# Two-block transformer on one core: the second block's element-wise work taken off POOL, the next heads projected ahead, gates moved forward, meta keys padded

## The chip, the cores and the metric

The kernel runs on one core of one Trainium2 chip. A core has five engines that work side by side, each through its own queue in order: PE (TensorE, matmul), DVE (VectorE), ACT (ScalarE), POOL (GpSimd) and SP (SyncE, here only the issuer of transfers). An engine that waits for one instruction's inputs holds everything queued behind it. The metric is the time of one execution on the device, in microseconds (us).

## The reference, cut to what matters

Two transformer blocks over 256 tokens and a width of 1024 in float32. The first (a mixer with banded attention and retention, then an MLP) keeps its instructions. The second prepends 16 learned meta tokens, projects once by `w_in`, and joins two kinds of attention by gates:

```python
def second_block(x, meta_tokens, pre_mix_gain, w_in, ...):
    h = jnp.concatenate([filler, meta, x], axis=1)
    ...
        u = rms_norm(h, pre_mix_gain[l])
        proj = u @ w_in[l]
        qa, ka, va, qb, kb, vb, g = jnp.split(proj, SPLITS, axis=-1)
        qa = rope(qa.reshape(B, Lp, SWA_Q_HEADS, HEAD_DIM), pos)
        ka = rope(ka.reshape(B, Lp, SWA_KV_HEADS, HEAD_DIM), pos)
        qb = rope(qb.reshape(B, Lp, DIFF_HEADS, 2, HEAD_DIM), pos)
        kb = rope(kb.reshape(B, Lp, DIFF_HEADS, 2, HEAD_DIM), pos)
        o_swa = windowed_gqa_sink_attention(qa, ka, va, attn_sink[l], pos, is_real)
        ...
        o_diff = differential_attention(qb, kb, vb, lam, ...)
        gates = jax.nn.sigmoid(g + b_gate[l])
        g_swa, g_diff = gates[..., :D_MODEL], gates[..., D_MODEL:]
        merged = g_swa * (o_swa @ w_branch_swa[l]) + g_diff * (o_diff @ w_branch_diff[l])
        h = h + rms_norm(merged @ w_out[l], post_mix_gain[l])
        ...
```

A gated feed-forward layer follows. The banded attention (16 query heads of 64, 4 key heads) lets a query see keys within 128 positions, all 16 meta keys, and a sink logit without a value: softmax over `[band, meta, sink]`. The differential attention (8 heads of two halves) is `(softmax(q1 k1) - lam * softmax(q2 k2)) @ v` over all 272 keys, with a norm per head. `rope` turns each pair of half heads: `[x1 c - x2 s, x2 c + x1 s]`.

## The kernel before

**Weights and matmuls.** Every matmul of weights is done in three passes over two parts of each number (high by high, high by low, low by high). The weights come as a stream of 272 units of 1024x128 (512 KB, laid out as 128x1024). `fetch` (L286 to L305) brings one: a transfer on SP's queue into one of four `raw` buffers, two casts on ACT to `hi` (L302), two subtractions on DVE to `lo` (L304), into one of five pairs of buffers. The units are used in the order in which `pack_weights` lays them. A unit over 256 tokens is 24 matmuls of 256 columns (L459), over 272 tokens 24 of 272. Queries, gates and branch products take two units at a time, called a block below: 48 matmuls.

**Ropes.** `rope_T` (L495 to L517) copies the projection from PSUM on ACT (`t`, L506 or L508), issues four transfers on ACT's queue that swap the half heads (`sw<-t`, L510, L511), multiplies by the cosines on DVE (L512), multiplies the swapped tile by the sines (L513) and adds (L516) on `self.slow`, which is POOL in the second block (set at L927) and DVE in the first. Keys are tiles of 128x272, queries of 128x512. `stack_q` (L519 to L528) splits the queries into high parts (ACT) and low parts (`self.slow`, L526, L527); `stack_k` (L529 to L544) does so for keys (`ks` on ACT, `kl` on DVE at L541 and on POOL at L542).

**Banded attention** (loop at L980): four chunks `c` of four heads, two query tiles each, so eight calls of `sink_attention` (L599 to L638). Per head: two score matmuls `s<-ks` and `s<-kl`; one matmul of 128 columns in bf16 that adds the mask (L566); on DVE the sink is copied into column 272 (L577) and the minimum taken (L571; queries are scaled by -0.125, so the minimum is the largest logit); exponentials with their sum on ACT (L581); reciprocal and scaling on DVE (L583, L584) to `pn`. Per tile of four heads: transposes (L620), a split into high and low (L331 with L330 on ACT), products `o_ps` (L624), with the third key tile of 16 rows only, then `ol` on ACT (L629), `of` on DVE (L631) and the split of the result into `os_t`. A second form, `sink_softmax1` (L586), which the first block uses, adds the mask and takes the minimum in one custom DVE instruction (L591) and scales on ACT (L597).

**Differential attention** (L990 to L1055): four pairs `pr` of heads; each begins with `keys()` (two units, two key tiles) and the queries, and ends with one gate block of the first kind (L1055). **Branches** (L1061 to L1072): four blocks `bs` on the banded result, then four times a gate block of the second kind (L1068) and a block `bd` on the differential result (L1069), their sum on POOL (L1071) and a split into `m2t`. The output projection `op` follows at 687 us, then the feed-forward layer.

**What sets the order.** The code is written out head by head, and a scheduler orders each engine's queue from it when the kernel is built, within the buffers that each tile has (`BUFS`) and the PSUM banks (`ROT`). That order is fixed.

## Time and profile before

| what | value |
|---|---|
| time, median of 3 runs | 903.83 us (902.67 to 905.01) |
| the profiled execution, its own time | 906.26 us |
| its span, first to last instruction | 904.5 us |
| PE busy in the span | 881.3 us, 97% |
| DVE busy | 628.5 us, 69% |
| ACT busy | 521.4 us, 58% |
| POOL busy | 152.8 us, 17% |
| mean granted clock of PE | 0.994 |

Shares over the whole span mix stages with different limits. The stages that the change touches lie between 426 us (first key projection of the second block) and 687 us (first output projection), and are read apart below. A busy PE is not PE at its peak: the records of its matmuls overlap, so their paces are read from long rows of equal matmuls in the chain.

### The profile page before, as it was taken

The page shows a single profiled execution, that of the slowest core. Times are in us where ns is not written, and L with a number is a line of the kernel's source. Part 1 is how long each engine was busy: PE and PEld are TensorE (multiplying, and loading weights), DVE is VectorE, ACT ScalarE, POOL GpSimd, SP SyncE. Part 2 cuts the span into 40 slices and gives each one's busy share as a digit, 9 for nine tenths or more (in the row PEclk, how much of TensorE's full clock was granted, in tenths as well). Part 3 has the DMA queues.
Part 4 walks back from the last instruction along what each step waited for, and adds up shares of the span by engine and source line. Part 5 has one row for each costly group of instructions (what it writes and reads, how often), then busy time and mean ns, then how long its engine had stood idle before and what let it go on. Part 6 is the DMA issues. An engine that isn't in the chain of part 4 may idle for free.

```text
span 904.5 us, 16459 instructions
## 1 busy us (share of the span) xinstructions
PE 881.3 (97%) x6172; PEld 812.4 (90%) x6172; DVE 628.5 (69%) x1203; ACT 521.4 (58%) x1145; POOL 152.8 (17%) x174
## 2 busy tenths in 40 slices
PE   7999999999999999999989999999999999999997
PEld 5899999998899999978978888889998799999996
DVE  5567798768655555665699999988666776656654
ACT  4644389546654444555657778887455554444542
POOL 2001110110011111111464525461110100000000
PEclk9999999999999999999989999999999999999999
DMA  8665754468476655654653343434467576655641
GB/s 294 221 211 167 216 163 154 146 211 305 161 218 192 194 186 189 207 189 148 187 168 98 112 131 108 138 107 133 147 185 241 180 231 188 187 186 187 188 162 46
DMA packets 48320, 160.25 MB, mean 177 GB/s; under 512 B 6497, under 2 KB 8417, under 8 KB 48242
## 3 DMA queue, kind: packets, MB, share of 16 engines
q1 hardware_dynamic: 43378, 153.49, 53.3%
q10 hardware_dynamic: 4672, 5.20, 2.1%
q8 instruction: 48, 0.79, 0.4%
q0 software_dynamic: 192, 0.52, 0.2%
q14 instruction: 30, 0.25, 0.1%
HBM read 151.38 MB, written 2.10 MB: 170 GB/s over the span
## 4 chain that ended last, share of the span: by engine, by line
PE 37%; DVE 8%; DMA 2%; ACT 2%; issue 1%; POOL 1%; ACTq 0%; POOLq 0%; DVEq 0%
PE fi_ps L459 13%; PE op L471 6%; PE gate_ps L459 4%; DVE lo L304 3%; PE bd_ps L459 2%; PE bs_ps L459 2%; PE q_ps L459 2%; PE k_ps L459 2%; DMA raw<-in_wstream_dram 2%; PE o_ps L624 1%; DMA sw<-t 1%; ACT hi L302 1%; PE pt_ps L620 1%; PE fi_ps L481 1%; PE s L563 1%
## 5 line engine op out<-in xcount | busy, mean ns | idle before, releaser
L304 DVE TENSOR_TENSOR lo<-raw,hi 128x512 fp32r<-128x512 f32 x536 | 372.8, 736 | 188.9 <-ACT hi L302 183.8
L302 ACT CAST hi<-raw 128x512 fp32r<-128x512 f32 x532 | 301.9, 618 | 229.2 <-issue 82.1
L471 PE MATMUL op<-hi,hid 128*128 128x512 f32 x416 | 128.9, 390 | 0.0
L459 PE MATMUL fi_ps<-xf2t,hi 128*128 128x256 f32 x640 | 114.4, 281 | 0.0
L459 PEld LDWEIGHTS fi_ps<-xf2t,hi 128*128 128x128 f32 x640 | 99.1, 188 | 0.9
L459 PE MATMUL fi_ps<-xf2t,lo 128*128 128x256 f32 x320 | 90.0, 281 | 0.0
L471 PEld LDWEIGHTS op<-hi,hid 128*128 128x128 f32 x416 | 76.3, 188 | 14.6
L471 PE MATMUL op<-lo,hid 128*128 128x512 f32 x208 | 81.1, 392 | 0.0
L459 PE MATMUL f_ps<-xf1t,hi 128*128 128x256 f32 x448 | 80.5, 281 | 0.0
L459 PEld LDWEIGHTS f_ps<-xf1t,hi 128*128 128x128 f32 x448 | 69.9, 189 | 1.2
L459 PE MATMUL f_ps<-xf1t,lo 128*128 128x256 f32 x224 | 63.0, 281 | 0.0
L459 PEld LDWEIGHTS fi_ps<-xf2t,lo 128*128 128x128 f32 x320 | 60.6, 189 | 0.0
L459 PE MATMUL q_ps<-x2t,hi 128*128 128x256 f32 x256 | 51.6, 292 | 0.0
L459 PE MATMUL gate_ps<-x2t,hi 128*128 128x256 f32 x256 | 48.7, 284 | 0.0
L459 PE MATMUL gate_ps<-x1t,hi 128*128 128x256 f32 x256 | 47.1, 283 | 0.0
L471 PEld LDWEIGHTS op<-lo,hid 128*128 128x128 f32 x208 | 39.0, 188 | 8.6
L459 PEld LDWEIGHTS f_ps<-xf1t,lo 128*128 128x128 f32 x224 | 42.4, 189 | 0.1
L459 PEld LDWEIGHTS q_ps<-x2t,hi 128*128 128x128 f32 x256 | 41.6, 194 | 0.7 <-issue 0.5
L853 POOL TENSOR_TENSOR sq<-relu 128x512 f32<-128x512 f32 x14 | 15.8, 1132 | 150.5 <-ACT relu L850 150.5
L419 POOL TENSOR_SCALAR e<-ss 128x1 f32<-128x1 f32 (+1 forms) x11 | 3.4, 312 | 220.1 <-ACT py L1092 191.8
L459 PEld LDWEIGHTS gate_ps<-x2t,hi 128*128 128x128 f32 x256 | 40.0, 189 | 0.5 <-issue 0.5
L459 PEld LDWEIGHTS gate_ps<-x1t,hi 128*128 128x128 f32 x256 | 39.6, 189 | 0.2
(323 smaller groups left out, 2008.2 us busy)
## 6 DMA issues: line engine op xcount, KB each, us to landing
raw<-in_wstream_dram SPq DMA_DIRECT2D x272, 512.0 KB, 3.7
sw<-t ACTq DMA_DIRECT2D x40, 64.0 KB, 4.0
x<-in_x_dram SPq DMA_DIRECT2D x3, 512.0 KB, 6.0
sw<-t ACTq DMA_DIRECT2D x40, 34.0 KB, 2.1
sw<-t ACTq DMA_DIRECT2D x8, 128.0 KB, 4.8
g_pre<-in_gains_dram SPq DMA_DIRECT2D x2, 512.0 KB, 7.0
...
```

What stands on the lines that cost most here:

```text
L302: nc.scalar.copy(hi[:, c:c + PIECE], raw[:, c:c + PIECE])
L304: nc.vector.tensor_sub(lo[:, c:c + PIECE], raw[:, c:c + PIECE], hi[:, c:c + PIECE].bitcast(F32))
L419: nc.gpsimd.tensor_scalar(out=e[:np_], in0=ss[:np_, 0:1], scalar1=1.0 / D, scalar2=EPS, op0=ALU.mult, op1=ALU.add)
L459: nc.tensor.matmul(out, wv[a][:, k, j * P:(j + 1) * P], XT[:, b, k, n0:n1], start=(i == 0), stop=(i == last))
L471: nc.tensor.matmul(out, XT[:, b, k0 + k, t0:t1], wv[a][:, k, c0:c0 + cn], start=(start and i == 0), stop=(stop and i == last))
L481: nc.tensor.matmul(out, XT[:, b, kn * j + k, t0:t1], ws[j][a][:, k, :cn], start=(i == 0), stop=(i == len(seq) - 1))
L563: nc.tensor.matmul(out, q, k[0][:, k0:k1], start=True, stop=False)
L620: nc.tensor.transpose(b[:kn, h, :], pn[:, h, k0:k0 + kn], self.ident)
L624: nc.tensor.matmul(o, vs[i][:kn, c, :], pt[:kn, x], start=(i == 0 and x == 0), stop=(i == len(ktiles) - 1 and x == 1))
L853: nc.gpsimd.tensor_tensor(out=q, in0=r, in1=r, op=ALU.mult)
```

## The change

- `self.slow` stays DVE in the second block, so the S-product and the sum of each rope and the low halves of the queries are on DVE. Half of the keys' low parts (`kl`, L542) stay on POOL.
- The banded attention uses the form of the first block: masks are a table `masks2` (128x544, one transfer on SP), added to the scores in the custom instruction that also takes the minimum; the mask matmuls, the sink copies and the separate minimum go; the scaling of `pn` goes from DVE to ACT. POOL copies the sinks (128x4 per tile).
- Queries of the next chunk, and keys and queries of the next pair, are projected one ahead; `ks` and `kl` get eight buffers for six.
- The first two gate blocks of the first kind stand ahead of the last banded chunk instead of in pairs 0 and 1; the four of the second kind stand ahead of the `bs` products, into tiles that the `pt` tiles used. The last sum goes from POOL to DVE.
- The third key tile is filled with zeros to 128 rows (tiles `va` and, for the transposed weights, `ptm`, cleared once by two memsets on POOL).

The diff, without imports, plain renames and context:

```diff
-    "b2": dict(vt=4, sw=2, t1=2, t2=2, ks=6, kl=6, qe=2, qo=2, p=6, a=2, at=1, atm=2, y=1, pn=2, pt=2),
-    "b3": dict(gt=4),
+    "b2": dict(sw=2, t1=2, t2=2, ks=8, kl=8, qe=2, qo=2, p=6, a=2, at=1, atm=2, y=1, pn=2, pt=2),
...
+
+    def kq(p):
+        in_a(w_in2, o_kb + 256 * p)
+        in_a(w_in2, o_qb + 256 * p)
+    in_a(w_in2, o_qa)
     for c in range(4):
-        in_a(w_in2, o_qa + 256 * c)
+        if c < 3:
+            in_a(w_in2, o_qa + 256 * (c + 1))
+        else:
+            kq(0)
+            in_a(w_in2, o_g)
+            in_a(w_in2, o_g + 256)
         if c == VB1:
             in_a(w_in2, o_vb + 512)
             in_a(w_in2, o_vb + 768)
     for p in range(4):
-        in_a(w_in2, o_kb + 256 * p)
-        in_a(w_in2, o_qb + 256 * p)
-        in_a(w_in2, o_g + 256 * p)
+        if p < 3:
+            kq(p + 1)
+        if p > 1:
+            in_a(w_in2, o_g + 256 * p)
+    for g in range(4):
+        in_a(w_in2, o_g + 1024 + 256 * g)
     for g in range(4):
         in_a(w_bs, 256 * g)
     for g in range(4):
-        in_a(w_in2, o_g + 1024 + 256 * g)
         in_a(w_bd, 256 * g)
     for g in range(4):
...
+    add("masks2", np.concatenate([z, le, z[:, :NMETA], ge, z, z[:, :NMETA]], axis=1))
...
-        mk = self.wp.tile([P, UC], F32, tag="raw", bufs=4, name="mk")[:, 0:2 * P]
-        a, n = cc["masks"]
-        nc.sync.dma_start(out=mk, in_=io["consts"][:, a:a + n])
-        self.identb = cp.tile([P, P], BF16, name="identb")
-        self.masks = cp.tile([P, 2 * P], BF16, name="masksb")
-        nc.gpsimd.tensor_copy(self.identb, self.ident)
-        nc.gpsimd.tensor_copy(self.masks, mk)
...
-        nc.tensor.matmul(out, q, k[1][:, k0:k1], start=False, stop=(mask is None))
-        for i, (mi, c0) in enumerate(mask or ()):
-            nc.tensor.matmul(out[:, c0:c0 + P], self.identb, self.masks[:, mi * P:(mi + 1) * P],
-                             start=False, stop=(i == len(mask) - 1))
+        nc.tensor.matmul(out, q, k[1][:, k0:k1], start=False, stop=True)
...
-    def sink_softmax(self, s, n, nsink, out):
-        nc = self.nc
-        nc.vector.tensor_copy(s[:, n:n + 1], nsink)
-        nm = self.row_min(s)
-        p = self.t([P, NKEY + 2], "p")
-        den = self.sm(1, "den")
-        nc.scalar.activation(out=p[:, :n + 1], in_=s, func=AF.Exp, bias=nm, scale=-1.0, accum_out=den)
-        rc = self.sm(1, "rc")
-        nc.vector.reciprocal(rc, den)
-        nc.vector.tensor_scalar(out=out, in0=p[:, :n], scalar1=rc, scalar2=None, op0=ALU.mult)
-
-    def sink_softmax1(self, s, n, mask, nsink, p):
+    def sink_softmax(self, s, n, mask, nsink, p):
...
-    def sink_attention(self, q, kst, vs, sink, ktiles, masks, OT, c, qt):
...
-        if isinstance(masks, list):
-            pn = self.t([P, 4, n], "pn")
-            for h in range(4):
-                s = self.sbank([P, n + 1], "s")
-                self.scores(s[:, :n], q[h % 2][:, h // 2, qt * P:(qt + 1) * P], kst, 0, n, masks)
-                self.sink_softmax(s, n, sink[:, 4 * c + h:4 * c + h + 1], pn[:, h, :])
-        else:
-            pn = self.t([P, 4, n + 1], "pn")
-            nc.gpsimd.tensor_copy(pn[:, :, n], sink[:, 4 * c:4 * c + 4])
-            for h in range(4):
-                s = self.sbank([P, n], "s")
-                self.scores(s, q[h % 2][:, h // 2, qt * P:(qt + 1) * P], kst, 0, n)
-                self.sink_softmax1(s, n, masks, sink[:, 4 * c + h:4 * c + h + 1], pn[:, h, :])
+        pn = self.t([P, 4, n + 1], "pn")
+        nc.gpsimd.tensor_copy(pn[:, :, n], sink[:, 4 * c:4 * c + 4])
+        for h in range(4):
+            s = self.sbank([P, n], "s")
+            self.scores(s, q[h % 2][:, h // 2, qt * P:(qt + 1) * P], kst, 0, n)
+            self.sink_softmax(s, n, mask, sink[:, 4 * c + h:4 * c + h + 1], pn[:, h, :])
         o = self.pv([P, 4, P], "o_ps")
         for i, (k0, kn) in enumerate(ktiles):
             b = self.tp([P, 4, P], "pt_ps")
             for h in range(4):
                 nc.tensor.transpose(b[:kn, h, :], pn[:, h, k0:k0 + kn], self.ident)
-            pt = self.t([P, 2, 4, P], "pt", F32R)
+            pt = self.t([P, 2, 4, P], "pt", F32R) if kn == P else self.ptm[qt]
             self.split(pt[:kn, 0], pt[:kn, 1], b[:kn])
             for x in range(2):
-                nc.tensor.matmul(o, vs[i][:kn, c, :], pt[:kn, x], start=(i == 0 and x == 0),
+                nc.tensor.matmul(o, vs[i][:, c, :], pt[:, x], start=(i == 0 and x == 0),
                                  stop=(i == len(ktiles) - 1 and x == 1))
         of = self.t([P, 2, P], "of")
-        if isinstance(masks, list):
-            ol = self.t([64, 4, P], "ol")
-            nc.scalar.copy(ol, o[64:128])
-            for e in range(2):
-                nc.vector.tensor_add(of[64 * e:64 * e + 64], o[0:64, e:4:2], ol[:, e:4:2])
-        else:
-            for e in range(2):
-                r = slice(64 * e, 64 * e + 64)
-                nc.scalar.copy(of[r], o[64:128, e:4:2])
-                nc.vector.tensor_add(of[r], o[0:64, e:4:2], of[r])
+        for e in range(2):
+            r = slice(64 * e, 64 * e + 64)
+            nc.scalar.copy(of[r], o[64:128, e:4:2])
+            nc.vector.tensor_add(of[r], o[0:64, e:4:2], of[r])
...
-        self.slow = nc.gpsimd
         rope_b = self.load("rope_b", [P, 2 * NKEY])
+        mk = self.load("masks2", [P, 2 * NKEY], rp)
+        mk = [mk[:, 0:NKEY], mk[:, NKEY:]]
...
-        vat = self.bp.tile([P, 3, 4, P], F32R, tag="A", name="va")
+        vat = self.bp.tile([P, 7, 4, P], F32R, tag="A", name="va")
+        nc.gpsimd.memset(vat[:, 0].bitcast(F32), 0.0)
+        nc.gpsimd.memset(vat[:, 3:7].bitcast(F32), 0.0)
+        self.ptm = [vat[:, 3:5], vat[:, 5:7]]
...
-                f = self.t([P, NKEY], "vt")
+                f = self.t([P, NKEY], "vt", tag="kl")
...
-            va[i] = v
+            va[i] = vat[:, i]
...
+        def queries():
+            return self.stack_q(self.rope_T(self.proj_a(XT, name="q_ps"), 2, NTOK, rope_b, 32, scale=-0.125))
+
         OS = self.big("C", 8, "os_t", NKEY)
         MS = self.bp.tile([P, 8, NTOK], F32, tag="D", name="ms")
         self.banks("WINDOW")
         ka = keys()
+        qn = queries()
         for c in range(4):
-            q = self.stack_q(self.rope_T(self.proj_a(XT, name="q_ps"), 2, NTOK, rope_b, 32, scale=-0.125))
+
+            q = qn
+            if c < 3:
+                qn = queries()
+            else:
+                kn = keys()
+                qn = queries()
+                for g in range(2):
+                    self.gate(XT, 16, g, MS[:, 2 * g:2 * g + 2, :])
             for qt in range(2):
-                self.sink_attention(q, ka[c], va, self.nsink[:, 8:24], kts, [(0, P)] if qt == 0 else [(1, 0)],
-                                    OS, c, qt)
+                self.sink_attention(q, ka[c], va, self.nsink[:, 8:24], kts, mk[qt], OS, c, qt)
...
         for pr in range(4):
-            kb = keys()
-            q = self.stack_q(self.rope_T(self.proj_a(XT, name="q_ps"), 2, NTOK, rope_b, 32, scale=-0.125))
+            kb, q = kn, qn
+            if pr < 3:
+                kn = keys()
+                qn = queries()
...
-            self.gate(XT, 16, pr, MS[:, 2 * pr:2 * pr + 2, :])
-        es.close()
-        es = ExitStack()
-        self.use(es.enter_context(self.phase("b3")), "b3")
+            if pr > 1:
+                self.gate(XT, 16, pr, MS[:, 2 * pr:2 * pr + 2, :])
...
+        gts = [self.t([P, 2, 4, P], "gd", tag="pt") for _ in range(2)]
+        gts = [t.rearrange("p a b c -> p (a b c)").rearrange("p (g m n) -> p g m n", g=2, m=2) for t in gts]
+        for gq in range(4):
+            self.gate(XT, 24, gq, gts[gq // 2][:, gq % 2])
...
         for gq in range(4):
-            tg = self.t([P, 2, 2, NTOK], "gt")
-            self.gate(XT, 24, gq, tg[:, 0])
+            tg = gts[gq // 2][:, gq % 2]
             b = self.proj_a(OD, name="bd_ps")
-            nc.vector.scalar_tensor_tensor(out=tg[:, 1], in0=tg[:, 0], scalar=1.0, in1=b, op0=ALU.add, op1=ALU.mult)
-            nc.gpsimd.tensor_tensor(out=tg[:, 0], in0=tg[:, 1], in1=MS[:, 2 * gq:2 * gq + 2, :], op=ALU.add)
-            self.split(MT[:, 0, 2 * gq:2 * gq + 2, 0:NTOK], MT[:, 1, 2 * gq:2 * gq + 2, 0:NTOK], tg[:, 0], 0.5)
+            nc.vector.scalar_tensor_tensor(out=tg, in0=tg, scalar=1.0, in1=b, op0=ALU.add, op1=ALU.mult)
+            nc.vector.tensor_add(tg, tg, MS[:, 2 * gq:2 * gq + 2, :])
+            self.split(MT[:, 0, 2 * gq:2 * gq + 2, 0:NTOK], MT[:, 1, 2 * gq:2 * gq + 2, 0:NTOK], tg, 0.5)
```

What this does to the queues, at three places. First POOL, where the second block's first ropes stand: `sw`, `t` are the S-product and the sum, `qe`, `qo` the low halves of queries, `kl` those of keys. Before:

```order
L513 TENSOR_TENSOR sw<-sw,rope_b 128x512
L516 TENSOR_TENSOR t_5068<-t_5068,sw 128x512
L513 TENSOR_TENSOR sw<-sw,rope_b 128x512
L516 TENSOR_TENSOR t_5332<-t_5332,sw 128x512
L526 TENSOR_TENSOR qe<-t_5068,qe 64x512
L527 TENSOR_TENSOR qo<-t_5068,qo 64x512
L513 TENSOR_TENSOR sw<-sw,rope_b 128x512
L526 TENSOR_TENSOR qe<-t_5332,qe 64x512
L527 TENSOR_TENSOR qo<-t_5332,qo 64x512
```

After, from the first sink copies on:

```order
L595 COPY pn<-nsink 128x4 x2
L548 TENSOR_TENSOR kl<-t_4922,ks 64x272 x2
L548 TENSOR_TENSOR kl<-t_4978,ks 64x272 x2
L595 COPY pn<-nsink 128x4
L548 TENSOR_TENSOR kl<-t_5994,ks 64x272
L595 COPY pn<-nsink 128x4
L548 TENSOR_TENSOR kl<-t_5994,ks 64x272
L595 COPY pn<-nsink 128x4 x2
```

Only the sink copies, the `kl` and (not shown) the `rq` of the differential heads are left there.

Next DVE in the first chunk, near the third query rope. `lo` are weight units, `s`, `mn`, `rc`, `pn` the softmax. Before:

```order
L512 TENSOR_TENSOR t_5596<-t_5597,rope_b 128x512
L304 TENSOR_TENSOR lo_5986<-raw_5987,hi_5985 128x512 x2
L577 COPY s<-nsink 128x1 x2
L571 TENSOR_REDUCE mn<-s 128x1
L577 COPY s<-nsink 128x1
L304 TENSOR_TENSOR lo_6219<-raw_6220,hi_6218 128x512
L571 TENSOR_REDUCE mn<-s 128x1 x2
L304 TENSOR_TENSOR lo_6219<-raw_6220,hi_6218 128x512
L583 RECIPROCAL rc<-den 128x1 x3
```

After (`ISA` with `masks` is the custom instruction, the one behind it reads its minimum):

```order
L582 ISA pn,mn<-s,masks_4679,nsink 128x272
L582 ISA mn 128x1
L532 TENSOR_TENSOR qe<-t_5148,qe 64x512
L582 ISA pn,mn<-s,masks_4679,nsink 128x272
L582 ISA mn 128x1
L533 TENSOR_TENSOR qo<-t_5148,qo 64x512
L582 ISA pn,mn<-s,masks_4679,nsink 128x272
L582 ISA mn 128x1
L317 TENSOR_TENSOR lo_5874<-raw_5875,hi_5873 128x512
L519 TENSOR_TENSOR sw<-sw,rope_b 128x512
L317 TENSOR_TENSOR lo_5909<-raw_5910,hi_5908 128x512 x2
L587 RECIPROCAL rc<-den 128x1
```

The low halves and the S-product now stand between the heads' softmax on DVE; the copies, minima and scalings are gone.

Last PE in the banded heads. Before, where pair 0's keys begin (`masksb` is the mask matmul):

```order
L563 MATMUL s<-ks,qo 128x272
L564 MATMUL s<-kl,qo 128x272
L566 LDWEIGHTS identb
L566 MATMUL s<-masksb,identb 128x128
L459 MATMUL k_ps<-x2t,hi_6218 128x272
L563 MATMUL s<-ks,qe 128x272
L564 MATMUL s<-kl,qe 128x272
L566 LDWEIGHTS identb
L566 MATMUL s<-masksb,identb 128x128
```

After, in the third chunk:

```order
L604 MATMUL pt_ps<-ident,pn 128x128 x4
L569 MATMUL s<-ks,qe 128x272
L570 MATMUL s<-kl,qe 128x272
L604 MATMUL pt_ps<-ident,pn 16x128 x4
L604 MATMUL pt_ps<-ident,pn 128x128 x3
L569 MATMUL s<-ks,qo 128x272
L570 MATMUL s<-kl,qo 128x272
L604 MATMUL pt_ps<-ident,pn 128x128
L569 MATMUL s<-ks,qe 128x272
L570 MATMUL s<-kl,qe 128x272
L569 MATMUL s<-ks,qo 128x272
L570 MATMUL s<-kl,qo 128x272
```

The mask matmuls are gone. Before, projections stand between the heads' scores; after, this piece holds scores, transposes and products alone. The projections of pair 0 and the first gates stand ahead of the last chunk.

## Rows read from the trace of the kernel before

**Rows 1.** Stretches: length; busy PE, PEld, DVE, ACT, POOL; clock; DMA; GB/s.

```profile
426.00:492.00 66.00, 62.62 (x475) 59.60 (x473) 54.22 (x105) 40.91 (x94) 29.18 (x23) 0.95 0.56 172
492.00:584.00 92.00, 88.42 (x645) 78.45 (x645) 87.87 (x201) 74.09 (x184) 43.94 (x38) 1.00 0.40 117
584.00:647.50 63.50, 61.00 (x520) 59.94 (x519) 50.82 (x119) 44.14 (x137) 19.49 (x20) 1.00 0.39 122
647.50:687.20 39.70, 39.70 (x338) 39.70 (x337) 25.41 (x35) 20.52 (x39) 4.83 (x3) 1.00 0.61 185
687.20:904.00 216.80, 210.34 (x1390) 191.98 (x1388) 132.55 (x238) 103.70 (x213) 6.43 (x13) 0.99 0.56 180
```

**Rows 2.** Tile `os_t` on DVE: duration in ns, first and last start.

```profile
L331 DVE TENSOR_TENSOR os_t<-of,os_t x8: 403/424/1504, 492.0 to 584.1; 128x256 fp32r<-128x256 f32 x8
```

**Rows 3.** Chain that ended last, 640 to 700: start, length, matmuls.

```profile
647.62 5.67 PE bd_ps L459 x48
653.29 5.68 PE gate_ps L459 x48
```

**Rows 4.** DVE groups, 426 to 647.5: count; busy, mean ns; idle before.

```profile
L304 DVE TENSOR_TENSOR lo<-raw,hi 128x512 fp32r<-128x512 f32 x97 | 81.2, 869 | 10.4 <-ACT hi L302 10.3
L584 DVE TENSOR_SCALAR pn<-p,rc 128x272 f32<-128x272 f32 x32 | 15.7, 518 | 0.2
...
L571 DVE TENSOR_REDUCE mn<-s 128x1 f32<-128x273 f32 x32 | 13.1, 428 | 0.1
...
L577 DVE COPY s<-nsink 128x1 f32<-128x1 f32 x32 | 4.3, 148 | 0.4 <-PE s L566 0.4
```

**Rows 5.** DVE groups, 50 to 130, the first block.

```profile
L513 DVE TENSOR_TENSOR sw<-sw,rope_a 128x512 f32<-128x512 f32 x2 | 1.4, 688 | 2.2 <-DMA sw<-t 2.2
...
L591 DVE CUSTOM_DVE_ANT_0 pn<-s,masks,nsink 128x256 f32<-128x256 f32 x1 | 0.5, 481 | 0.0
```

**Rows 6.** Timeline of DVE, 457 to 467: start, length.

```profile
460.80 1.79 DVE L512 TENSOR_TENSOR t<-t,rope_b 128x512 f32<-128x512 f32 x1
```

**Rows 7.** Timeline of POOL in the same window.

```profile
460.41 1.64 POOL L513 TENSOR_TENSOR sw<-sw,rope_b 128x512 f32<-128x512 f32 x1
```

**Rows 8.** Timeline of DVE, 415 to 425; idle before in brackets.

```profile
419.25 4.91 DVE L304 TENSOR_TENSOR lo<-raw,hi 128x512 fp32r<-128x512 f32 x8 [4.26 <-ACT hi L302]
```

**Rows 9.** Timeline of DVE at the first and the eighth `os_t`.

```profile
490.40 0.63 DVE L584 TENSOR_SCALAR pn<-p,rc 128x272 f32<-128x272 f32 x2
...
584.82 0.44 DVE L512 TENSOR_TENSOR t<-t,rope_b 128x272 f32<-128x272 f32 x1 [0.27 <-ACT t L506]
```

**Rows 10.** POOL groups, 426 to 647.5.

```profile
L542 POOL TENSOR_TENSOR kl<-t,ks 64x272 fp32r<-64x272 f32 x20 | 19.2, 960 | 14.2 <-ACT ks L539 13.4
L513 POOL TENSOR_TENSOR sw<-sw,rope_b 128x512 f32<-128x512 f32 x8 | 12.4, 1548 | 29.2 <-DMA sw<-t 15.7 <-DVE pt L331 5.6 <-PE od_ps L1038 3.9
...
L1047 POOL TENSOR_TENSOR rq<-ms,nhalf 128x2 f32<-128x2 f32 x8 | 5.8, 729 | 31.9 <-DVE ms L1045 31.9
```

**Rows 11.** ACT groups, 110 to 150, the first block.

```profile
L597 ACT ACTIVATE pn<-pn,rc 128x256 f32<-128x256 f32 x5 | 2.4, 504 | 0.1
```

**Rows 12.** Timeline of PE, 534.3 to 536, around a product of 16 rows.

```profile
534.89 0.28 PE L459 MATMUL gate_ps<-x2t,lo 128*128 128x256 f32 x1
535.10 0.49 PE L624 MATMUL o_ps<-pt,va 16*128 16x512 f32 x1
535.52 0.50 PE L459 MATMUL gate_ps<-x2t,hi 128*128 128x256 f32 x2
```

**Rows 13.** Timeline of PE, 577 to 582: the last banded product.

```profile
580.24 0.50 PE L624 MATMUL o_ps<-pt,va 16*128 16x512 f32 x1
```

**Rows 14.** Waits of DVE, 50 to 130: us, times, longest.

```profile
DVE sw L513 <- DMA sw<-t: 7.7, 5, 2.2
```

**Rows 15.** Stretches around a low clock, columns as in the first group.

```profile
460.00:467.00 7.00, 4.99 (x40) 4.67 (x38) 7.00 (x9) 2.11 (x6) 6.69 (x5) 1.00 0.32 98
467.00:475.00 8.00, 7.34 (x35) 6.69 (x36) 6.85 (x24) 4.38 (x16) 0.10 (x1) 0.57 0.62 196
```

More of the change, by code (lines that the diff above doesn't have):

```diff
@@ L11 @@
 F32R = mybir.dt.float32r
-BF16 = mybir.dt.bfloat16
 AF = mybir.ActivationFunctionType
```

8 lines of the change are left out of this document (5 added, 3 removed).

## The prediction

> **What bounds the kernel now.** I read the busy time by stretch first [rows 1]. The change lies between 426 and 687 us: banded attention with the key and query projections (to the eighth split of its output `os_t`, 584.1 us [rows 2]), differential attention, and the branch products up to 687.2. What follows, 687 to 904, and all before 426 keep their instructions. From 492 to 584 DVE is busy 87.87 of 92.00 us, 95.5%, with 201 instructions; PE's 88.42 there is overlapped records, not matmuls at their pace. Summing every matmul between 426 and 687 at its pace (0.118 us for 256 columns, 5.68/48 in [rows 3], larger ones in proportion) gives about 241 us of PE work in 261.2, so PE loses about 20. It loses none in 647.5 to 687.2, where PE is busy throughout [rows 1] and the chain is `gate` and `bd` blocks of 48 matmuls back to back [rows 3]. So the middle has two bounds in turn: DVE until banded attention is done, then PE.
>
> Why DVE is full is in the groups. `lo` takes 869 ns over 97 instructions [rows 4], where an undisturbed 128x512 two-operand instruction takes 688 [rows 5]. The timeline shows why: `t` of 128x512 took 1.79 us at 460.80 while POOL's `sw` ran 1.64 us from 460.41 [rows 6, 7]. The excess is 97 x 0.18 = 18 us in `lo`, 32 x (0.518 - 0.355) = 5 us in `pn` (0.355 is its duration undisturbed, below), and some 13 us over the other groups compared in the same way: about 36 us of stall between 426 and 647.5, 14.4, 16.3 and 6.7 us in the three stretches. POOL is busy 29.18 + 43.94 + 19.49 = 92.6 us there [rows 1], so a POOL microsecond costs DVE about 0.39.
>
> **The change part by part.** Records of one engine overlap: eight `lo` in a row took 4.91 us [rows 8], 0.60 each against durations of 0.68, so a pitch is the duration less 0.08.
>
> *POOL's work goes to DVE.* Per rope the S-product and the sum, per query the two low halves. That is 8 ropes of 512 columns, 10 of 272, and 16 low halves: 32 x 0.60 [rows 5] + 20 x 0.35 (0.44 less 0.08 [rows 9]) = 26.2 us more on DVE. POOL keeps 20 `kl` of 0.96 and 8 `rq` of 0.73 [rows 10], 25 us, so stalls fall from 36 to 0.39 x 25 = 10. The two cancel almost exactly.
>
> By the row of one instruction instead of this mean, each `kl` would hold DVE for its whole 0.96 us; that is a rival below. The Trainium skill, "SBUF — State Buffer", section "Who interferes with whom", says that a DVE instruction with two SBUF inputs contends with a GpSimd instruction that reads SBUF and that the lock is held for the whole instruction. The 1.79 us agrees with that; the mean of 0.39 says that few of POOL's instructions meet such a partner for their whole length.
>
> *Mask, sink and minimum in one instruction, scaling to ACT.* Gone from DVE are 32 `s` copies (0.07), 32 `mn` reductions (0.35) and 32 `pn` scalings ((0.63 - 0.08)/2 = 0.275, the pair undisturbed in [rows 9]): 22 us. Instead come 32 custom instructions of 272 columns; 256 took 481 ns in the first block [rows 5], so 0.42 at the pitch: 13.6 us. DVE's net over both parts is 26.2 - 22 + 13.6 = 17.9 us, less 26 of stalls: -8. ACT gains 32 scaled copies; the 256-wide one takes 504 ns [rows 11], about 0.42 at the pitch: 13.3 us, 14.5 with the split of `of` into two.
>
> *PE loses little.* 32 mask matmuls of 128 columns go, about 0.06 each: 1.8 us. The padding of the 16 meta-key rows makes the 16-row products full. The 16-row product starts 0.21 us after the matmul before it and holds the next one 0.42 [rows 12], against 0.118 and 0.236: 0.28 each, 16 of them, 4.6 us. I take both as gone; if the pause belongs to something else, 4.6 us of PE comes back, much of it under DVE's cover. The two memsets stand on POOL ahead of the last `sq` of the first block, whose inputs come later than POOL is free: nothing.
>
> *The order.* Counting the schedule between markers at these pitches: **to the first `os_t`** DVE has 36.1 us of work before and 56.2 after. Ten more `lo` (6.0), nine S-products and nine sums (8.8), eight low halves (4.8), one more query and key rope with two `kl` (1.7), 16 custom instructions (6.8) and small ones (0.9) come in, and 13 reductions, 12 scalings and 14 copies (8.9) leave. With projecting ahead, the second chunk's queries stand before the first chunk's products. **First to eighth `os_t`:** 69.4 before, 71.8 after: two `lo`, 20 scalings, 18 reductions and 18 copies go, 16 custom instructions, 6 low halves and 17 rope instructions come. The count before, times 1.03, plus 16.3 of stalls is 87.8, the busy time in the row [rows 1], so the count carries. **PE from the last banded product (580.2 us [rows 13]) to the first `bd` (647.6):** 63.5 before, 78.1 after. 133 more matmuls of 256 columns (181 of gates, less 48 of queries) at 0.118 are 15.7, and 13 key matmuls less take 1.6 off, and four scores more add 0.5. **`bd` to `op`:** 39.7 before, 22.7 after, since three gate blocks (17.0 us, [rows 3]) have gone forward.
>
> *The sum.* In 426 to 492 DVE idles 66 - 54.2 = 11.8 us; it gets 20.1 x 1.03 = 20.7 more work, 12 us less stall (2 of the 14.4 stay, for six `kl`), and I let its idle shrink to about 7, since the projections now feed it earlier: the first `os_t` comes at 492 + 20.7 - 12.4 - 4.5 = 496. Then 71.8 x 1.03 = 74 plus 6 of stalls is 80, at the present share of 95.5% it is 83.8: the eighth `os_t` at 579.8, 4.3 us earlier than 584.1, and the last banded product, four us ahead of it, likewise. From there PE is the bound: 78.1 plus 1.5 lost, since gate matmuls now fill the gaps between the differential heads, against 67.4 now (63.5 and 3.9 lost), 12.2 more; then 22.7 plus 0.3 against 39.7, 16.7 less. Together -4.3 + 12.2 - 16.7 = **-8.8 us** at `op`; the rest is as before. The profiled run took 906.26 us with a span of 904.5, the median is 903.83; I take the difference off the median: **895 us**.
>
> **The rivals.** *Better, about 884.* The order interleaves so well that half of PE's loss goes too: PE's work falls to 235 us, so with 6 us lost instead of 17 the middle ends 11 us earlier still. For it: 94 gate matmuls and the next keys lie between the banded heads. Against it: PE's order has a stretch with scores, transposes and products only, where DVE has 20 us of work for 12 of PE's.
>
> *No change, 901 to 906.* ACT becomes co-bound. It was busy 74.09 of 92 [rows 1]; it gets 17 scaled copies for its share (7 us) and loses some exponentials and casts, 76.4, and with about 3.5 us of transfer issues 80 of 84. A head now goes PE, DVE, ACT, DVE, ACT, PE, four hand-offs between two engines that are both full. If the share of DVE drops from 95.5 to 88%, 80 takes 91 us and 7 of the 8.8 are gone. With each of the 12 `kl` in this stretch at 0.96 instead of 0.37 us DVE has 7 us more, 87/0.955 = 91, and the time is 902; I give this 0.04 of the chance below. The same range holds the case that the stall does not come from POOL but from DVE's own full queue: then 16 us stay, 90/0.955 = 94, about 905.
>
> *Slower, about 910.* The S-product on DVE waits for the swapped halves, which come by transfer (`sw<-t`), and DVE works in order: `lo`, the softmax and every split queue behind it, and PE behind those. In the first block, where DVE does it already, DVE waited five times, 7.7 us in all [rows 14], for six ropes of 512 columns: 1.3 each. 18 ropes would be 23 us. It decides against the change once such waits before the eighth `os_t` exceed 8.8 us, and passes the 0.3% beyond 11.5; 23 us less the 8.8 and what runs under PE's cover gives 910 and up to 917. Against it: one chunk or pair is projected ahead, so the order puts other DVE work between the transfer's issue and the S-product. POOL waits for these transfers now, 15.7 us before the 512-wide `sw` alone [rows 10], and little queues behind it.
>
> One more cost lies in the range: the granted clock was 0.57 on the mean in 467 to 475, so that PE ran at 1.2 instead of 2.4 GHz for most of it, 0.43 x 8 = 3.4 us lost at the most [rows 15], after a thin stretch (4.99 of 7 us busy in 460 to 467). The thin stretch of the new order could bring a second such fall, and the first may go.
>
> **How the numbers follow.** About 0.3%, 2.7 us either way of 903.83 (901.1 to 906.5), is what a measurement can tell from no change. Forecast 888.5 to 901: 0.60. Better, near 884: 0.12. No change, 901 to 906.5: 0.16. Slower, near 910: 0.12. So faster 0.72, same 0.16, slower 0.12. Eight in ten: from 886, inside the better case, to 905, inside the no-change case.
>
> **What would show it.** Right: `lo` near 0.72 instead of 0.87 us; POOL's busy time in the middle near 26; the first `os_t` at 494 to 498, the eighth at 577 to 583; four `bd` blocks back to back in 22.7 us; `op` at 676 to 681. Wrong: DVE idle before `sw` for the transfer of over 9 us in all; `lo` still at 0.85; ACT over 95% busy in the banded stretch with DVE waiting for `p`; PE idle or at half clock between the eighth `os_t` and `bd`.

## The result, and the profile after

The changed kernel took 897.84 us (897.41 to 898.27, 3 runs) against 903.83 before: a ratio of 0.9935, 95% interval 0.9916 to 0.9953, 6.0 us less. Timed again with more runs (below) it was 0.9921, 0.9904 to 0.9939, 896.94 against 904.23, 7.3 us less. The forecast was 895, -8.8 us, in a range of 886 to 905. The profiled execution took 897.84 us with a span of 895.9, 8.6 less than the span before.

Busy time by stretch, with the bounds at the first and the eighth `os_t`, the first `bd` and `op`, as in [rows 1]; columns are length, then busy PE, PEld, DVE, ACT and POOL with counts, granted clock, DMA share and GB/s:

```profile
426.00:504.50 78.50, 77.76 (x630) 76.34 (x629) 64.41 (x144) 60.28 (x143) 6.15 (x8) 1.00 0.56 179
504.50:591.80 87.30, 78.19 (x577) 71.81 (x577) 78.27 (x191) 78.00 (x195) 17.04 (x16) 0.98 0.39 122
591.80:655.80 64.00, 64.00 (x551) 63.78 (x550) 48.20 (x121) 44.96 (x137) 9.26 (x10) 1.00 0.41 133
655.80:678.50 22.70, 22.70 (x195) 22.70 (x194) 16.62 (x26) 11.04 (x19) 0.00 (x0) 1.00 0.57 185
678.50:895.30 216.80, 210.13 (x1390) 191.98 (x1388) 132.15 (x239) 103.46 (x213) 5.40 (x12) 1.00 0.54 180
```

The last stretch is as long as before (216.8), and from the first key projection (426.0 us before, 426.8 after) to `op` it took 251.7 us instead of 261.2, so the difference lies there. The stretch of the `bd` blocks went from 39.7 to 22.7 us. The chain there answers to [rows 3]: start, length, matmuls.

```profile
655.92 22.72 PE bd_ps L465 x192
```

192 matmuls in 22.72 us, 0.118 each, without a gap. From the last banded product to there PE has no gap either: that product is the last line below (timeline of PE, [rows 13] before), so the tail takes 655.9 - 577.6 = 78.3 us, where the count of matmuls at their pace was 78.1.

```profile
577.60 0.39 PE L608 MATMUL o_ps<-va 128*128 128x512 f32 x1
```

The heads ahead of it are another matter. PE by stretches of 10 us:

```profile
520.00:530.00 10.00, 7.88 (x57) 6.86 (x56) 9.33 (x25) 7.94 (x21) 1.11 (x2) 1.00 0.57 189
530.00:540.00 10.00, 7.45 (x50) 6.23 (x48) 6.53 (x22) 9.83 (x27) 0.19 (x1) 1.00 0.11 30
540.00:550.00 10.00, 7.54 (x38) 5.90 (x38) 9.48 (x28) 9.15 (x26) 3.65 (x4) 0.83 0.17 55
```

Here PE is busy 22.9 of 30 us by the records, and some 19 at the pace of its matmuls; the clock fell to 0.83 in the last slice. DVE and ACT together fill the stretch, one or the other is busy 29.2 of the 30 us, each with a gap while the other works: ACT is at 9.83 of 10 where DVE has 6.53.

DVE's groups from 424 to 650 (count; busy, mean ns; idle before them), to be laid beside [rows 4]:

```profile
L317 DVE TENSOR_TENSOR lo<-raw,hi 128x512 fp32r<-128x512 f32 x108 | 71.8, 697 | 6.3 <-ACT hi L315 6.1
L582 DVE CUSTOM_DVE_ANT_0 pn<-s,masks,nsink 128x272 f32<-128x272 f32 x32 | 14.9, 491 | 0.5 <-PE s L570 0.3
...
L547 DVE TENSOR_TENSOR kl<-t,ks 64x272 fp32r<-64x272 f32 x20 | 11.2, 560 | 0.3
...
L519 DVE TENSOR_TENSOR sw<-sw,rope_b 128x272 f32<-128x272 f32 x10 | 4.4, 436 | 9.5 <-DMA sw<-t 9.4
```

`lo` fell from 869 to 697 ns: nearly all of the stall is gone. In its place stands the last line's idle time, 9.5 us of waiting for the swapped halves. DVE's waits in 426 to 592 (us, times, longest):

```profile
DVE sw L519 <- DMA sw<-t: 10.9, 6, 3.4
DVE lo L317 <- ACT hi L315: 4.2, 5, 1.6
DVE pt L344 <- ACT pt L343: 3.6, 2, 3.3
```

POOL's groups from 424 to 650 ([rows 10] before):

```profile
L548 POOL TENSOR_TENSOR kl<-t,ks 64x272 fp32r<-64x272 f32 x20 | 23.1, 1154 | 62.8 <-ACT ks L545 31.1 <-issue 23.5 <-PE s L570 7.0
L1043 POOL TENSOR_TENSOR rq<-ms,nhalf 128x2 f32<-128x2 f32 x8 | 7.5, 934 | 53.0 <-DVE ms L1041 44.2 <-ACT ks L545 8.7
```

### The profile page after: what moved, and what is told of

Same layout as the page of the kernel before. It is cut to its first block, busy times and chain, and to the rows that moved or that the text cites. A ratio compares the mean times of both kernels' runs of the same rounds, so it can differ in the third digit from the quotient of the medians.

```text
span 895.9 us, 16370 instructions
## 1 busy us (share of the span) xinstructions
PE 870.4 (97%) x6140; PEld 808.4 (90%) x6140; DVE 615.9 (69%) x1227; ACT 535.6 (60%) x1185; POOL 87.9 (10%) x126
## 5 line engine op out<-in xcount | busy, mean ns | idle before, releaser
L317 DVE TENSOR_TENSOR lo<-raw,hi 128x512 fp32r<-128x512 f32 x536 | 352.3, 696 | 177.9 <-ACT hi L315 170.9
L465 PE MATMUL gate_ps<-x2t,hi 128*128 128x256 f32 x256 | 50.6, 285 | 0.0
L465 PE MATMUL q_ps<-x2t,hi 128*128 128x256 f32 x256 | 47.2, 282 | 0.0
L465 PEld LDWEIGHTS q_ps<-x2t,hi 128*128 128x128 f32 x256 | 39.7, 188 | 0.3 <-ACT t L512 0.2
L465 PE MATMUL gate_ps<-x2t,lo 128*128 128x256 f32 x128 | 36.4, 284 | 0.0
L465 PE MATMUL gate_ps<-x1t,lo 128*128 128x256 f32 x128 | 36.2, 283 | 0.0
```

The costliest lines, as they stand in the source:

```text
L317: nc.vector.tensor_sub(lo[:, c:c + PIECE], raw[:, c:c + PIECE], hi[:, c:c + PIECE].bitcast(F32))
L465: nc.tensor.matmul(out, wv[a][:, k, j * P:(j + 1) * P], XT[:, b, k, n0:n1], start=(i == 0), stop=(i == last))
```

## The experiments

Each kernel is timed beside runs of the kernel before on the same chip; those had medians of 903.5 to 904.4 us, so two rows can differ by 0.9 us for that reason alone. Beside the times stands one number that I worked out from the trace of the profiled execution as the prediction did: PE time lost between 426 us and `op`, which is the wall time less the sum of all matmuls at their paces (the products of 16 rows at the pace of 128).

| kernel | median us | against 896.94 | PE lost, us |
|---|---|---|---|
| before | 903.83 | +6.9 | 24.8 |
| changed, again | 896.94 | | 15.9 |
| POOL's work back on POOL | 907.71 | +10.8 | 26.2 |
| key ropes alone back on POOL | 900.33 | +3.4 | 17.4 |
| before, with POOL's work on DVE | 907.51 | +10.6 | 25.5 |
| no padding | 899.33 | +2.4 | 17.6 |
| gates back | 901.90 | +5.0 | 19.6 |
| nothing projected ahead | 900.47 | +3.5 | 21.0 |
| scaling back on DVE | 899.56 | +2.6 | 19.9 |
| last `kl` on DVE too | 900.30 | +3.4 | 20.6 |
| four gate blocks ahead of the last chunk | 897.17 | +0.2 | 14.4 |
| two ahead of the third, two of the last | 896.77 | -0.2 | 15.3 |
| no swap transfers | 886.57 | -10.4 | 4.7 |

A profiled execution can lie up to 2.5 us off its median (902.05 us with the scaling back on DVE, 898.66 with the key ropes on POOL); the times of the profiled executions follow PE's loss to within 2 us. Except where the text says so the scheduler laid out each variant's queues anew, so differences of 2 or 3 us may come from the order as well as from the edit. Where gates or projections move, the order of the weights in `pack_weights` moves with them; that part of the diffs is left out. Masks, sinks and minimum in one instruction were not taken back by themselves.

**The changed kernel again.** No edit.

> The changed kernel as it is, timed again in more rounds. The result had a median of 897.84 us, 6.0 less than before, while the two profiled executions lie 8.4 apart (906.26 and 897.84). Theory 1: before has a half-clock stretch (0.57 on the mean in 467 to 475 us of its profile) only in some executions, the profiled one among them; then the medians differ by 6.0 +- 0.7 again, and runs of before spread by more than those of the changed kernel. Theory 2: the three runs fell high or low by chance; then the medians differ by 8 to 9 us.

896.94 us over 6 runs against 904.23 over 18. Neither theory is shown: the difference of the medians is 7.3, between the two. The profiled execution of before, 906.26 us, lay 2.4 us over the median of the first three runs and 2.0 over that of the 18; runs of before went from 902.89 to 907.68 with mean clocks from 0.988 to 0.999, and the slowest had the lowest clock, but runs at 0.994 took 902.96 and 907.40. So the clock is at most part of the spread.

**POOL's work, in both directions.** First the changed kernel with one line put back:

```diff
+        self.slow = nc.gpsimd
         rope_b = self.load("rope_b", [P, 2 * NKEY])
```

> The changed kernel with the ropes' S-product and sum and the queries' low halves on POOL again, all else as changed. Theory (the prediction's sum): DVE loses 26.2 us of work and gets 26 us of stalls back, so the two cancel: 898 +- 3 us, with DVE's lo near 0.85 us instead of 0.70, and POOL near 90 us busy in the middle. Rival: POOL was the cause of the loss in the banded heads, since its instructions take 1.0 to 1.6 us in the path of the next heads: 903 to 907 us.

907.71 us, a ratio to before of 1.0040 (1.0025 to 1.0056). The rival's side, just above its range: the move is worth 10.8 us with the rest of the change in place, not nothing. `lo` is at 825 ns, as the theory had it (DVE, 424 to 660):

```profile
L317 DVE TENSOR_TENSOR lo<-raw,hi 128x512 fp32r<-128x512 f32 x108 | 85.4, 825 | 12.9 <-ACT hi L315 11.9 <-PE pt_ps L604 0.6
```

Laid against the groups of the changed kernel, DVE's instructions are some 25 us longer for 61.7 us more of POOL, 0.40 per POOL us, so the price of the stall was right. What the theory left out is where the stall falls. POOL's timeline for one pair's queries; on DVE a pair of `a`, the difference of two softmaxes of a differential head, once with POOL idle and once beside it; and the matmul on PE that waited:

```profile
588.43 0.92 DVE L1015 SCALAR_TENSOR_TENSOR a<-p,rl 128x272 f32<-128x272 f32 x2
...
591.66 1.34 POOL L519 TENSOR_TENSOR sw<-sw,rope_b 128x512 f32<-128x512 f32 x1 [1.04 <-ACT ks L545]
593.08 1.10 POOL L548 TENSOR_TENSOR kl<-t,ks 64x272 fp32r<-64x272 f32 x1
594.25 1.38 POOL L522 TENSOR_TENSOR t<-t,sw 128x512 f32<-128x512 f32 x1
595.71 2.12 POOL L548 TENSOR_TENSOR kl<-t,ks 64x272 fp32r<-64x272 f32 x1
597.90 1.36 POOL L532 TENSOR_TENSOR qe<-t,qe 64x512 fp32r<-64x512 f32 x1
599.34 1.26 POOL L533 TENSOR_TENSOR qo<-t,qo 64x512 fp32r<-64x512 f32 x1
...
599.31 1.99 DVE L1015 SCALAR_TENSOR_TENSOR a<-p,rl 128x272 f32<-128x272 f32 x2
...
601.04 0.30 PE L1022 MATMUL at_ps<-ident,a 128*128 128x128 f32 x1 [2.62 <-DVE a L1015]
```

From the S-product at 591.66 to the end of `qo` at 600.60 are 8.9 us, of which the four instructions of this rope are 5.3 and `kl` that stand between them 3.2; on DVE the four take 0.6 each. The matmul at 601.04 did not wait for this rope, since its `a` began at 599.31, ahead of `qo`. It waited for the pair of `a` itself, which took 1.99 us beside `qo` instead of 0.92. PE stood 2.62 us, and its granted clock was 0.83 in 600 to 610. Of the 10.3 us that PE loses more than in the changed kernel, some 8 lie behind the last banded product: 4.1 in 580 to 600 and 3.0 after, for instance, where the changed kernel loses 0.4. What the length of the way through POOL costs by itself is not shown.

Then the kernel before with this part alone:

```diff
-        self.slow = nc.gpsimd
         rope_b = self.load("rope_b", [P, 2 * NKEY])
```

> The kernel before with only this part of the change: ropes' S-product and sum and queries' low halves on DVE. Theory: 26 us of work for 26 us of stalls, 904 +- 3 us, lo near 0.70 us. Rival (the prediction's slower case): without projecting ahead DVE waits for the swapped halves, over 9 us before the eighth os_t, and the time is 907 to 915 us.

907.51 us, 1.0031 (1.0010 to 1.0052): slower by 3.3, at the lower end of the rival's range. `lo` fell to 716 ns, and DVE waited for transfers instead:

```profile
DVE sw L513 <- DMA sw<-t: 8.6, 6, 3.3
```

That these waits are the 3.3 us is not shown: 6.8 of the 8.6 lie ahead of 465 us, while PE loses more than before at 550 to 560 (5.4 us against 0.9) and at 640 to 660 (4.5 against none), there waiting for `y` of the last heads.

So the part that is worth 10.8 us inside the change costs 3.3 by itself, and the rest of the change without it costs 3.5 (907.71 against 904.23). The parts do not add up.

**The padding.** The products take 16 rows again, and the two memsets go (not shown); the order of the second block's queues is unchanged:

```diff
-                nc.tensor.matmul(o, vs[i][:, c, :], pt[:, x], start=(i == 0 and x == 0),
+                nc.tensor.matmul(o, vs[i][:kn, c, :], pt[:kn, x], start=(i == 0 and x == 0),
```

> The changed kernel with the third key tile's products of 16 rows again (no zeros, no memsets); the order of all instructions is the same. The prediction counts 0.28 us for each of 16 products, 4.6 us of PE. Theory 1: they lie in the banded heads, where PE has 15 us of idle pace (73.5 us of matmuls in 88.3), and are mostly hidden: 898 to 899.5 us. Theory 2: PE pays them in full: 902.4 us.

899.33 us, 2.4 more (intervals to before 0.9919 to 0.9959 here, 0.9904 to 0.9939 with padding, so they overlap). That is in the range of theory 1, at its upper end: by the medians about half of the 4.6 us reaches the end.

**The gates.** All eight blocks back to their places: one of the first kind per pair, those of the second kind ahead of each `bd`.

```diff
-                for g in range(2):
-                    self.gate(XT, 16, g, MS[:, 2 * g:2 * g + 2, :])
...
-            if pr > 1:
-                self.gate(XT, 16, pr, MS[:, 2 * pr:2 * pr + 2, :])
+            self.gate(XT, 16, pr, MS[:, 2 * pr:2 * pr + 2, :])
...
-        for gq in range(4):
-            self.gate(XT, 24, gq, gts[gq // 2][:, gq % 2])
...
             tg = gts[gq // 2][:, gq % 2]
+            self.gate(XT, 24, gq, tg)
```

> The changed kernel with the gates where they were: first kind one per differential pair, second kind ahead of each branch product on the differential result. Theory (two bounds in turn): after the last banded product PE is full anyway, so it matters only how much PE work there is ahead of it; there the schedule holds 132.9 us of matmuls against 134.3, so 897 to 900 us. Rival (gates as filler are the gain): PE loses between the differential heads again, as before (3.9 us there), and the gates' 11.4 us are missing under the banded heads: 903 to 909 us.

901.90 us, 5.0 more: above the theory's range and below the rival's. PE loses 3.7 us more, spread over the heads (2.2 more up to 500 us, 1.9 in 500 to 520, 1.8 after 600), less in 520 to 550.

**Projecting ahead.** Queries and keys in front of the heads that use them:

```diff
-            q = qn
-            if c < 3:
-                qn = queries()
-            else:
-                kn = keys()
-                qn = queries()
+            q = queries()
...
-            kb, q = kn, qn
-            if pr < 3:
-                kn = keys()
-                qn = queries()
+            kb = keys()
+            q = queries()
```

> The changed kernel without projecting ahead: queries of a chunk, keys and queries of a pair stand in front of the heads that use them; gates and all else as changed. Theory 1 (projecting ahead is what hides the transfers of the swapped halves from DVE's queue): DVE waits for the transfers over 15 us in all instead of 10.6, 904 to 909 us. Theory 2 (the scheduler moves the projections ahead by itself within the buffers): 897 to 900 us.

900.47 us, 3.5 more, just above the range of theory 2. DVE's wait for transfers rose only from 10.6 to 12.9 us: the scheduler moves most projections forward by itself. But 8.0 us of these waits now lie in 500 to 580, where it was 2.9. Theory 1 has fallen as the main use of projecting ahead.

**More gates as filler.** If PE merely lacks work in 520 to 550, two more gate blocks there should fill it:

```diff
-                for g in range(2):
+                for g in range(4):
                     self.gate(XT, 16, g, MS[:, 2 * g:2 * g + 2, :])
```

> The changed kernel with all four gate blocks of the first kind ahead of the last banded chunk instead of two. PE's pace in the changed kernel is lost only in the banded heads, 11 us of it between 520 and 550 us, where nothing but scores, transposes and products is left; two blocks are 11.4 us of PE work and 4.8 us of lo on DVE. Theory 1 (DVE has room there, 64.3 of 73.1 us busy): 889 to 893 us. Theory 2 (DVE and ACT together are the bound, the blocks' lo and hi delay the heads): 895 to 899 us.

897.17 us, no change. The other placing:

> The changed kernel with the four gate blocks of the first kind spread, two ahead of the third banded chunk and two ahead of the fourth. Same two theories as for four ahead of the fourth: 888 to 893 us, or 895 to 899; if the place decides (the pace is lost from 520 us on, in the third chunk), this one is the better of the two by 2 us or more.

896.77 us, no change, and the place decides nothing. The stretch was filled, and much of the loss came back behind it. Stretches of the changed kernel and of the one with four blocks ahead of the last chunk (the first key projection stands at 425.6 and at 428.3 us):

```profile
520.00:550.00 30.00, 23.87 (x147) 19.96 (x146) 25.46 (x75) 27.48 (x74) 5.47 (x7) 0.89 0.23 76
550.00:580.00 30.00, 28.65 (x226) 27.30 (x225) 28.65 (x62) 25.87 (x63) 8.16 (x6) 1.00 0.38 117
600.00:676.00 76.00, 76.00 (x651) 75.82 (x651) 54.91 (x122) 46.30 (x129) 6.45 (x7) 1.00 0.43 146
```

```profile
520.00:550.00 30.00, 26.95 (x203) 24.92 (x201) 23.37 (x65) 26.72 (x67) 1.56 (x4) 0.99 0.38 126
550.00:580.00 30.00, 28.75 (x205) 27.02 (x205) 29.24 (x66) 27.00 (x68) 10.05 (x9) 0.90 0.27 81
600.00:677.00 77.00, 75.14 (x625) 74.32 (x624) 57.45 (x137) 48.74 (x139) 8.03 (x10) 0.98 0.41 136
```

PE's busy time in 520 to 550 went from 23.9 to 27.0, but from the first key projection to the last banded product (583.2 instead of 575.6) it is now 155.0 us instead of 150.0: of the 11.4 us of added work some 6 filled gaps. The blocks are then missing at the end of the differential heads: 1.9 of 77 us not busy there, and at the matmuls' pace 4.5 us lost instead of 0.3, most of it at 655 to 661, where PE waits for the last head's `y`:

```profile
PE ot_ps L1047 <- DVE y L1043: 1.4, 1, 1.4
```

**Scaling and the last `kl`.** The scaling of `pn` on DVE again:

```diff
+        if n > 256:
+            nc.vector.tensor_scalar(out=p[:, :n], in0=p[:, :n], scalar1=rc, scalar2=None, op0=ALU.mult)
+        else:
-        nc.scalar.activation(out=p[:, :n], in_=p[:, :n], func=AF.Copy, scale=rc)
+            nc.scalar.activation(out=p[:, :n], in_=p[:, :n], func=AF.Copy, scale=rc)
```

> The changed kernel with the softmax scaling of the banded heads on DVE again (in place, 0.275 us at the pitch) instead of on ACT (0.43). In the changed kernel's trace ACT runs without a gap from 523 to 552 us, while DVE once waits 3.3 us for it. Theory 1 (ACT became the bound of the thin stretch, the prediction's no-change case in part): ACT loses 13.3 us of work, DVE gets 8.8, and the time falls to 892 to 895 us. Theory 2 (DVE is the bound, as the prediction has it): half of the 8.8 us falls into the banded stretch and the time rises to 900 to 902 us.

899.56 us, 2.6 more, just below the range of theory 2 and far from theory 1. In 500 to 580 ACT's busy time fell by 11 us, so ACT is not what bounds this stretch by itself; DVE's rose by 3:

```profile
500.00:580.00 80.00, 71.77 (x517) 65.37 (x516) 70.61 (x173) 72.61 (x182) 14.06 (x14) 0.96 0.37 117
```

```profile
500.00:580.00 80.00, 72.59 (x504) 66.19 (x503) 73.79 (x187) 61.62 (x154) 15.59 (x14) 0.91 0.33 103
```

And `kl` off POOL:

```diff
-            nc.gpsimd.tensor_tensor(out=kl[b], in0=kf[a], in1=ks[a].bitcast(F32), op=ALU.subtract)
+            nc.vector.tensor_sub(kl[b], kf[a], ks[a].bitcast(F32))
```

> The changed kernel with the last keys' low halves off POOL too, on DVE. POOL's 20 kl take 1.16 us each there, on DVE 0.36 at the pitch. Theory 1 (POOL's instructions still hold DVE, 0.39 us each, 0.39 x 23 = 9 us of stall against 7.2 us of work; and the keys are ready 0.7 us earlier): 894 to 897 us. Theory 2 (the remaining stalls are small: lo is at 0.70 against 0.68 us): DVE has 7 us more and the time is 898 to 901 us.

900.30 us, 3.4 more: theory 2. Without POOL the `lo` of 128x512 takes 682 ns, so what POOL still costs DVE in the changed kernel can be read by difference (DVE, 424 to 650):

```profile
L317 DVE TENSOR_TENSOR lo<-raw,hi 128x512 fp32r<-128x512 f32 x106 | 69.2, 682 | 6.3 <-ACT hi L315 6.2
...
L547 DVE TENSOR_TENSOR kl<-t,ks 64x272 fp32r<-64x272 f32 x20 | 8.6, 431 | 0.2
```

108 x 15 ns in `lo`, 20 x 129 ns in DVE's own `kl`, half a us in `t`: some 5 us for the 23 us of `kl` that POOL no longer does (it is busy 9.5 us instead of 32.5), 0.2 per POOL us and not 0.39.

**The swap transfers.** Left out, with the S-product on the unswapped copy:

```diff
-        for p in range(0, P, 2 * half):
+        for p in range(0, P if tn != NKEY else 0, 2 * half):
...
-        self.slow.tensor_tensor(out=sw, in0=sw, in1=S, op=ALU.mult)
+        self.slow.tensor_tensor(out=sw, in0=raw if tn == NKEY else sw, in1=S, op=ALU.mult)
```

> The changed kernel without the transfers that swap the half heads in the second block: the S-product reads the unswapped copy, so that part of the ropes is left out and nothing waits for a transfer. In the changed kernel DVE waits 10.6 us for these transfers between 426 and 600 us, 2.9 of it in 500 to 580. Theory 1 (most of the waits lie ahead of 500 us, where PE is full anyway): 894 to 897 us. Theory 2 (these waits are what the banded stretch still loses): 886 to 891 us.

886.57 us, 0.9812 (0.9796 to 0.9828) of before and 10.4 less than the changed kernel: theory 2, although DVE waits only 2.9 us of its 10.6 in 500 to 580. Both kernels, the changed one first, from 430 to 490 us and in the thin stretch:

```profile
430.00:490.00 60.00, 59.26 (x484) 58.40 (x484) 50.00 (x113) 44.59 (x104) 5.68 (x7) 1.00 0.55 175
520.00:550.00 30.00, 23.87 (x147) 19.96 (x146) 25.46 (x75) 27.48 (x74) 5.47 (x7) 0.89 0.23 76
```

```profile
430.00:490.00 60.00, 59.09 (x478) 57.86 (x477) 56.95 (x135) 52.62 (x128) 6.70 (x9) 1.00 0.43 143
520.00:550.00 30.00, 28.75 (x228) 27.45 (x226) 27.31 (x60) 29.52 (x73) 7.13 (x8) 1.00 0.29 90
```

In 430 to 490 PE is equally full in both, but DVE gets through 57.0 us of work instead of 50.0 and ACT through 52.6 instead of 44.6. Both gaps have the size of what the transfers take there: DVE waits 7.4 us for them, and their 32 issues hold ACT's queue for 18.3 us, 8.1 of them while none of ACT's instructions runs. Later the last banded product comes at 566.0 instead of 575.6, and PE loses 1.8 us instead of 11.0 in 520 to 550 (up to 3.3 of the 11.0 are the granted clock, 0.89 instead of 1.00). How such a wait comes about (changed kernel, ACT's copy and its transfer issues, then DVE):

```profile
477.55 0.37 ACT L512 COPY t<-k_ps 128x272 f32<-128x272 f32 x1
...
477.95 0.52 ACTq L516 DMA_DIRECT2D sw<-t  x1
...
478.50 0.60 ACTq L517 DMA_DIRECT2D sw<-t  x1
479.14 0.61 ACTq L516 DMA_DIRECT2D sw<-t  x1
479.78 0.61 ACTq L517 DMA_DIRECT2D sw<-t  x1
...
483.40 0.44 DVE L519 TENSOR_TENSOR sw<-sw,rope_b 128x272 f32<-128x272 f32 x1 [3.40 <-DMA sw<-t]
```

The copy of the keys starts at 477.55; the four issues follow one another on ACT's queue at 0.52 to 0.61 us each until 480.39; the halves are there at 483.40, and DVE has stood 3.40 us.

**Key ropes back on POOL.** If DVE's standing in its queue were the whole price, POOL could do the standing for the ten key ropes:

```diff
+        eng = nc.gpsimd if tn == NKEY and m == 1 else self.slow
-        self.slow.tensor_tensor(out=sw, in0=sw, in1=S, op=ALU.mult)
+        eng.tensor_tensor(out=sw, in0=sw, in1=S, op=ALU.mult)
...
-        self.slow.tensor_tensor(out=out, in0=t1, in1=sw, op=ALU.add)
+        eng.tensor_tensor(out=out, in0=t1, in1=sw, op=ALU.add)
```

> The changed kernel with the S-product and the sum of the ten key ropes (128x272) on POOL again; the queries' ropes and low halves stay on DVE. Without the swap transfers the time fell by 10 us, and in the changed kernel the longest waits of DVE for a transfer (3.5 and 1.7 us) stand ahead of key ropes, at 482 and 435 us. Theory 1 (such a wait, early, while PE is full, is paid later in the thin stretch; on POOL little queues behind it): DVE loses 6 of its 10.6 us of waits and 7 us of work and gets 0.39 x 20 = 8 us of stalls: 892 to 895 us. Theory 2 (POOL's way is longer by two instructions of 1.0 us and its instructions hold DVE's: the 10.8 us that all of POOL's work costs divide by the work): 900 to 902 us.

900.33 us, 3.4 more, theory 2, though DVE's waits did fall as meant:

```profile
DVE lo L317 <- ACT hi L315: 6.6, 9, 1.4
DVE os_t L344 <- ACT os_t L343: 3.0, 1, 3.0
DVE kl L548 <- ACT ks L546: 3.0, 2, 2.5
...
DVE sw L520 <- DMA sw<-t: 1.8, 3, 1.1
```

From 10.6 to 1.8 us for the transfers, but DVE waits more for `ks`, `os_t` and `hi` from ACT. So DVE's waits cannot be taken away at no price; what they cost alone this run does not show, since POOL's instructions hold DVE again (`lo` 722 ns instead of 697). The run without transfers prices the transfers as a whole: issue, landing, the waits and the order around them. Which of these carries the 10.4 us stays open; a kernel with fewer transfers for the same ropes was not run.

## Why the prediction was right, and where it was wrong

The size was right to within 3 us, and PE's part of the mechanism held: the tail was forecast at 78.1 plus 1.5 us and took 78.3, the `bd` blocks at 22.7 plus 0.3 and took 22.7, and `op`, forecast at 687.2 - 8.8 = 678.4, came at 678.5. PE lost 16.7 us up to there, 17 in the forecast. Before it lost 24.8, of which 4.6 are the products of 16 rows as counted. Of the signs named, `lo`, the `bd` blocks and `op` came as for right; the two marks of `os_t` and POOL's busy time did not, and one sign of being wrong came: DVE idle before `sw` for over 9 us (10.9).

Three steps did not hold.

*DVE's marks.* The first `os_t` came at 504.5 instead of 496, the eighth at 591.8 instead of 579.8. The term that failed is DVE's idle time up to the first `os_t`, set at 7 us "since the projections now feed it earlier". It was 78.5 - 64.4 = 14.1, 7.6 of it three waits for transfers. In the next stretch DVE was busy 78.3 of 87.3 us, 90%, not 95.5%: two engines that take turns with the heads and wait for each other (of the 9.0 us idle 5.4 are waits for ACT, 3.3 for transfers). That is the no-change case's mechanism, at less than its price. The time held all the same because the second step failed the other way: the last banded product was put four us ahead of the eighth `os_t`, and it came 14 us ahead (577.6 against 575.9 forecast). The split was simply placed late in DVE's queue, and nothing needs it before the `bs` blocks. The forecast tied PE's start of the tail to a mark that no longer stood for it. A mark 12 us late and a lead 10 us longer left an error of 1.7 us; that the two cancelled was luck.

Where the gain lies is not where the sum put it either. Up to the last banded product PE lost some 20.5 us before, 4.6 of them the products of 16 rows, and some 16.5 after; behind it some 4 before and 0.5 after. So PE waited under the banded heads about as long as before, some 16 us apart from those products: the change as a whole did not shorten that. What PE no longer loses is what was counted for the products of 16 rows, and the gaps between the differential heads, which the gates now fill.

*Stall against work.* The sum had 26.2 us of work and 26 us of stall cancel (the stall's three parts, 14.4, 16.3 and 6.7, make 37.4 and not 36, which changes little). The work came; the stall fell further than to the 10 us left in the sum, to some 5 by the run without POOL's `kl`; and yet the move costs 3.3 us by itself and gains 10.8 inside the change. A sum over DVE's time cannot show that, since it prices neither the transfers that DVE now waits for nor on which instructions the stall falls, such as the `a` that PE waited for. The runs fit that in the order of before the wait for transfers weighs more, and with the next heads projected ahead POOL's hold on the heads' own instructions; that each order turns the balance was measured, why it does was only argued. The prediction named both mechanisms, the first as the slower rival, but set its threshold wrongly: DVE waited 10.9 us for transfers before the eighth `os_t`, more than the 8.8 at which the gain was to be gone. Waiting under a full PE seems to cost only later, and not one for one.

*The median.* The difference of two profiled executions was taken off the median of before, though its profiled execution lay 2.4 us above that median. By spans the difference is 8.6, by medians 6.0 and 7.3.

The padding's 4.6 us were a PE sum; by the medians 2.4 arrived. POOL's remaining work, 25 us in the sum, was 32.5: `kl` and `rq` became 5.6 us longer, and the sink copies, 1.9, were not in it. The low clock that the prediction allowed for moved: it was 0.57 in 467 to 475 before and 1.00 there after, and 0.83 in 540 to 550 after.

The Trainium skill, "SBUF — State Buffer", section "Who interferes with whom", has the second engine blocked for a whole instruction. A single row agrees, the pair of `a` that took 1.07 us more beside a `qo` of 1.26. The averages are lower, 0.39 us of DVE per POOL us before and 0.2 for `kl` in the changed kernel; how many of POOL's instructions met one of DVE that they could hold was not counted.
